# Loading the experts' weights from SyncE's and ScalarE's DMA queues in turn, in place of SyncE's alone

## The chip, the cores and the metric

The kernel runs on one core of one Trainium2 chip. The metric is device time in microseconds (us) of one execution of the whole program. Engines are named as the profile names them: PE is TensorE's matmul (PEld its weight load), DVE is VectorE, ACT is ScalarE, POOL is GpSimd, SP is SyncE. A "q" behind an engine (SPq, ACTq) is the engine's own sequencer, where it waits and where it issues DMAs.

## The reference, cut to what matters

The program computes two transformer blocks on 512 tokens of width 1024. The change touches the first block's feed-forward part, a mixture of 16 experts in which each expert picks its 64 best tokens. All of it is float32.

```python
def expert_choice_ffn(h, w_router, w_gate, w_up, w_down):
    B, N, D = h.shape                               # 1, 512, 1024
    cap = EC_FACTOR * N // N_EXPERTS                # 64 tokens per expert
    aff = jax.nn.softmax((h @ w_router).astype(F32), axis=-1)
    gate, idx = lax.top_k(jnp.swapaxes(aff, 1, 2), cap)
    xg = jax.vmap(lambda hb, ib: hb[ib])(h, idx)
    hid = jax.nn.silu(jnp.einsum('becd,edf->becf', xg, w_gate)) * jnp.einsum('becd,edf->becf', xg, w_up)
    y = jnp.einsum('becf,efd->becd', hid, w_down) * gate[..., None].astype(h.dtype)
    return jax.vmap(lambda yb, ib: jnp.zeros((N, D), yb.dtype).at[ib.reshape(-1)].add(yb.reshape(-1, D)))(y, idx)
```

`w_gate` and `w_up` are 16 x 1024 x 2048 and `w_down` is 16 x 2048 x 1024, so the three hold 384 pieces of one megabyte (MiB).

## The kernel before, in words

**Order of the program.** First come the first block's mixers, the output projection with the router (matmuls `wo`, whose weights are split by ACT at L1812 into `wh` and by DVE at L1813 into `wl`), and the choice of tokens. Then come the experts (function `experts`), and then the second block. A scheduler puts the instructions of each engine into one fixed order, and each engine works through its own list strictly in that order: while an instruction waits for a semaphore, nothing behind it on that engine starts, and that holds for the issue of a DMA too.

**The experts** are taken two at a time, in eight pairs. The text counts the one-megabyte loads from 0 to 383. Pair p (0 to 7) uses loads 48p to 48p+47: 16 of `w_gate`, then 16 of `w_up`, then 16 of `w_down`, the two experts in turn. For one pair, the steps in order are:

1. gather the pair's tokens with matmuls (tile `g`, L1993), which ACT copies to `xg` (L1997); the first half stands before the gate matmuls, the rest among them;
2. 64 gate matmuls (tile `a`, L2025), then ACT applies Silu from PSUM to `hid` (L2038, four instructions);
3. 64 up matmuls (L2025 again, into the same four PSUM banks, so they wait for the Silu), which DVE multiplies into `hid` (L2040);
4. turn `hid` with transposes (L2046) and do 64 down matmuls (tile `y`, L2060);
5. ACT scales the result (`ysb`, L2069, two instructions), PE spreads it over the tokens (`o`, L2076 and L2077), DVE adds it up in `accT` (L2078). PE then gathers for the next pair.

In PE's list the `o` matmuls of a pair stand ahead of all matmuls of the next pair.

**The loads.** `Stream` gives each load the next buffer of a ring: 2 + 9 + 2 + 6 buffers, and one more from the pool `x2`, 20 in all. So load u needs the buffer that load u-20 had, and waits until PE has used that one up. There is a second condition. The landing of every DMA, of whatever queue, is counted on one of eight semaphores (DMAHW0 to DMAHW7) that the DMAs take in turn, and a DMA is issued only after the one eight places before it has landed. Both waits stand on the engine that issues. Before the change that is SP (L93), which has no other work. The second block's loads (L283) are on SP, and a few small ones (L116, L120, L1799, L2128, L2130) are on ACT's queue.

Of the kernel before, what the change touches and what calls it, by code (L numbers as in the profile page):

```python
# [40 lines left out]
class Ring:  # L41

    def __init__(self, *pools):
        self.order = [p for p in pools for _ in range(p[2])]
        self.i = 0
# [38 lines left out]
class Stream:  # L84

    def __init__(self, nc, ring, srcs):
        self.nc, self.ring, self.srcs, self.q = nc, ring, list(srcs)[::-1], []

    def ahead(self, n):
        for _ in range(n):  # L90
            src, a = self.srcs.pop()
            v = self.ring.next().rearrange("p (a b) -> p a b", a=a)
            self.nc.sync.dma_start(v, src)  # L93
            self.q.append(v)

    def next(self):
# [2068 lines left out]
```

## Time and profile before

| | |
|---|---|
| median of 3 runs | 2568.22 us (2567.2 to 2570.2) |
| the profiled execution's own time | 2567.43 us |
| its span, first to last instruction | 2565.7 us |
| mean granted TensorE clock | 0.987 of full speed |
| busy share of the span | PE 96%, PEld 65%, DVE 41%, ACT 27%, POOL 10% |
| bytes read from HBM | 543.56 MB, 213 GB/s over the span |

A share of busy time is an average over stages with different limits. PE's share is high nearly everywhere, because matmuls overlap in the records; what ends a wait in a stage tells more than the share. The experts take the span from about 570 to 1500 us.

### The profile page before, as it was taken

What the parts mean: (1) busy time and instruction counts of PE and PEld (TensorE: products, weight loads), DVE (VectorE), ACT (ScalarE), POOL (GpSimd) and SP (SyncE); (2) the same over time, 40 slices, a digit from 0 to 9 for tenths busy, and PEclk for the clock granted to TensorE, in tenths of its full rate; (3) what the DMA queues carried; (4) which work ended last, traced back from release to release, by engine and by line L of the source; (5) the groups of instructions that cost most, each with busy time, mean ns of one, the idle gap of its engine ahead of it and who ended that gap; (6) DMA issues with size and microseconds to landing.
All of it is one profiled execution on the core that took longest, in us unless ns stands there. A gap on an engine that the chain in (4) does not pass through costs nothing. (4 is left out here: it accounts for less than half of the span.)

```text
span 2565.7 us, 31621 instructions
## 1 busy us (share of the span) xinstructions
PE 2456.9 (96%) x12919; PEld 1660.6 (65%) x12919; DVE 1044.4 (41%) x1871; ACT 691.0 (27%) x1314; POOL 249.3 (10%) x304
## 2 busy tenths in 40 slices
PE   7988999989999999999999999999999999999999
PEld 5768878863434343433434358778888897788887
DVE  5699348633111101010101056744444556644443
ACT  4422337520001000000000045532222355322221
POOL 1344354200000000000000021000000020000000
PEclk9998999989999999999999999999999999999999
DMA  8441110469999999999999943133222221333220
GB/s 274 149 150 34 48 36 18 141 274 419 420 422 421 421 421 421 421 421 422 421 421 421 421 163 99 64 117 94 88 97 76 64 83 50 115 99 99 91 91 33
DMA packets 165432, 547.75 MB, mean 213 GB/s; under 512 B 19183, under 2 KB 100903, under 8 KB 113959
## 3 DMA queue, kind: packets, MB, share of 16 engines
q1 hardware_dynamic: 159120, 544.39, 54.8%
q10 hardware_dynamic: 6167, 1.33, 0.3%
q8 instruction: 102, 1.67, 0.3%
q14 instruction: 43, 0.35, 0.0%
HBM read 543.56 MB, written 2.13 MB: 213 GB/s over the span
## 5 line engine op out<-in xcount | busy, mean ns | idle before, releaser
L2025 PE MATMUL a<-w,xg 128*64 128x512 f32 x2048 | 498.3, 597 | 0.0
L2025 PEld LDWEIGHTS a<-w,xg 128*64 128x64 f32 x2048 | 179.0, 136 | 293.8 <-issue 282.6
L194 ACT ACTIVATE wh<-w 128x512 fp32r<-128x512 f32 (+3 forms) x304 | 202.6, 678 | 457.5 <-PE gu L201 223.5
L2060 PE MATMUL y<-w,hT 128*64 128x512 f32 x1024 | 266.9, 599 | 12.7 <-DMA w<-in_w_down_dram 9.6
L202 PE MATMUL gu<-hh,wl 128*128 128x512 f32 x704 | 278.0, 395 | 0.0
L201 PE MATMUL gu<-hl,wh 128*128 128x512 f32 x704 | 276.4, 393 | 0.0
L200 PE MATMUL gu<-hh,wh 128*128 128x512 f32 x704 | 274.0, 389 | 0.0
L195 DVE TENSOR_TENSOR wl<-w,wh 128x512 fp32r<-128x512 f32 (+3 forms) x304 | 223.6, 748 | 122.6 <-ACT wh L194 122.4
L2060 PEld LDWEIGHTS y<-w,hT 128*64 128x64 f32 x1024 | 90.5, 136 | 171.3 <-issue 131.0
L2040 DVE TENSOR_TENSOR hid<-a,hid 128x512 f32<-128x512 f32 x32 | 21.8, 690 | 331.4 <-PE a L2025 331.1
L201 PEld LDWEIGHTS gu<-hl,wh 128*128 128x128 f32 x704 | 132.5, 188 | 30.9
L200 PEld LDWEIGHTS gu<-hh,wh 128*128 128x128 f32 x704 | 132.5, 188 | 29.5
L202 PEld LDWEIGHTS gu<-hh,wl 128*128 128x128 f32 x704 | 132.7, 188 | 26.5
L2069 ACT ACTIVATE ysb<-y,wt 128x512 fp32r<-128x512 f32 x16 | 11.0, 688 | 505.9 <-PE y L2060 505.1
L200 PE MATMUL dn<-hid,wh 128*128 128x512 f32 x352 | 139.4, 401 | 0.0
L202 PE MATMUL dn<-hid,wl 128*128 128x512 f32 x352 | 137.7, 395 | 0.0
L201 PE MATMUL dn<-hid,wh 128*128 128x512 f32 x352 | 137.1, 394 | 0.0
L732 DVE TENSOR_TENSOR accT<-dn,accT 128x512 f32<-128x512 f32 x96 | 66.1, 690 | 125.8 <-PE dn L202 125.8
L241 POOL MEMSET gg<- 128x256 f32 x1 | 0.3, 312 | 929.0 <-PE y L2060 929.0
L1997 ACT ACTIVATE xg<-g,mT,sc 128x128 f32<-128x128 f32 x64 | 25.9, 454 | 208.2 <-PE g L1993 208.2
L2011 DVE COPY wt<-wt 64x1 f32<-64x1 f32 x16 | 2.5, 156 | 191.8 <-PE wt L2008 191.7
L201 PEld LDWEIGHTS dn<-hid,wh 128*128 128x128 f32 x352 | 66.1, 188 | 17.6 <-DVE hid L722 2.3
(694 smaller groups left out, 4057.0 us busy)
## 6 DMA issues: line engine op xcount, KB each, us to landing
w<-in_w_gate_dram SPq DMA_DIRECT2D x150, 1024.0 KB, 19.8
w<-in_w_up_dram SPq DMA_DIRECT2D x150, 1024.0 KB, 19.8
w<-in_w_down_dram SPq DMA_DIRECT2D x150, 1024.0 KB, 19.8
w<-in_w_mod_dram SPq DMA_DIRECT2D x24, 1024.0 KB, 8.9
w<-in_w_in_dram SPq DMA_DIRECT2D x16, 1024.0 KB, 5.3
w<-in_w_out_dram SPq DMA_DIRECT2D x8, 1024.0 KB, 5.0
wo<-in_w_out_dram SPq DMA_DIRECT2D x4, 1024.0 KB, 9.9
w<-in_w_in_dram SPq DMA_DIRECT2D x4, 576.0 KB, 3.8
```

Source lines behind the costliest of these rows:

```text
L194: nc.scalar.activation(hv, src, AF.Copy)
L195: (eng or nc.vector).tensor_tensor(lv, src, hv.bitcast(F32), op=OP.subtract)
L200: nc.tensor.matmul(out, a[0], b[0], start=start, stop=False)
L201: nc.tensor.matmul(out, a[0], b[1], start=False, stop=False)
L202: nc.tensor.matmul(out, a[1], b[0], start=False, stop=stop)
L732: nc.vector.tensor_tensor(xT[:, d], z, xT[:, d], op=OP.add)
L1997: nc.scalar.activation(xg[:, dd, :], g[:, d, :], AF.Identity, scale=k.sc2[:, dd:dd + 1], bias=k.mT[:, 0, 24 + dd:25 + dd])
L2011: nc.vector.tensor_copy(wt[64 * i:64 * i + 64], tp[64 * i:64 * i + 64, 0, i:i + 1])
L2025: nc.tensor.matmul(acc[f][64 * i:64 * i + 64, :], xg[:, kk, 64 * i:64 * i + 64], us[i][:, 0, f * 512:f * 512 + 512], start=kk == 0, stop=k ...
L2040: nc.vector.tensor_tensor(h, a, h, op=OP.mult)
L2060: nc.tensor.matmul(y[dh][64 * i:64 * i + 64, :], hT[g][:, j, 64 * i:64 * i + 64], us[i][:, r, dh * 512:dh * 512 + 512], start=g + j == 0, ...
L2069: nc.scalar.activation(yh, y[i], AF.Copy, scale=wt)
```

## The change

`Stream.ahead` now issues even loads from SP and odd loads from ACT. Sources, buffers, sizes and the order of the ring stay as they are.

```diff
 class Stream:
 
     def __init__(self, nc, ring, srcs):
-        self.nc, self.ring, self.srcs, self.q = nc, ring, list(srcs)[::-1], []
+        self.nc, self.ring, self.srcs, self.q, self.n = nc, ring, list(srcs)[::-1], [], 0
 
     def ahead(self, n):
         for _ in range(n):
             src, a = self.srcs.pop()
             v = self.ring.next().rearrange("p (a b) -> p a b", a=a)
-            self.nc.sync.dma_start(v, src)
+            (self.nc.sync, self.nc.scalar)[self.n % 2].dma_start(v, src)
+            self.n += 1
             self.q.append(v)
```

The change puts 192 DMA issues into ACT's list, among the work that it had. Lines behind 93 stand one higher in the changed kernel (L1812 is L1813 there). Three places show what that does to the lists.

SP in the middle of the experts, before: five loads in a row and the semaphores that each waits for. `PE` is the buffer, `DMAHW` the landing eight DMAs back.

```order
L93 DMA w<-in_w_gate_dram 128x2048 [waits DMAHW4_49,PE_49]
L93 DMA w<-in_w_gate_dram 128x2048 [waits DMAHW5_49,PE_49]
L93 DMA w<-in_w_gate_dram 128x2048 [waits DMAHW6_49,PE_49]
L93 DMA w<-in_w_gate_dram 128x2048 [waits DMAHW7_49,PE_49]
L93 DMA w<-in_w_gate_dram 128x2048 [waits DMAHW0_49,PE_49]
```

SP at a like place in the changed kernel:

```order
L93 DMA w<-in_w_gate_dram 128x2048 [waits DMAHW4_49,PE_49]
L93 DMA w<-in_w_gate_dram 128x2048 [waits DMAHW6_49,PE_49]
L93 DMA w<-in_w_gate_dram 128x2048 [waits DMAHW0_49,PE_49]
L93 DMA w<-in_w_gate_dram 128x2048 [waits DMAHW2_49,PE_49]
L93 DMA w<-in_w_gate_dram 128x2048 [waits DMAHW4_49,PE_49]
```

SP keeps the even loads and the even semaphores; the odd ones (DMAHW1, 3, 5 and 7) went with the odd loads to ACT, where each still waits for the landing of the load eight before it.

ACT from the Silu of one pair to that of the next, before (`xg`, `oht` and `hid` of pairs 2 and 3):

```order
L2038 ACTIVATE hid<-a 128x16x32 x4
L2069 ACTIVATE ysb<-y,wt 128x512 x2
L1997 ACTIVATE xg<-g,mT,sc_4944 128x128 x8
L2005 ACTIVATE oht<-tp 128x512
L2038 ACTIVATE hid<-a 128x16x32 x4
```

ACT over the same stretch of a pair in the changed kernel:

```order
L2039 ACTIVATE hid<-a 128x16x32 x4
L93 DMA w<-in_w_down_dram 128x2048 x7
L93 DMA w<-in_w_gate_dram 128x2048 x8
L93 DMA w<-in_w_up_dram 128x2048
L2070 ACTIVATE ysb<-y,wt 128x512 x2
L93 DMA w<-in_w_up_dram 128x2048
L1998 ACTIVATE xg<-g,mT,sc_4944 128x128 x4
L93 DMA w<-in_w_up_dram 128x2048 x2
L1998 ACTIVATE xg<-g,mT,sc_4944 128x128 x2
L93 DMA w<-in_w_up_dram 128x2048 x2
L1998 ACTIVATE xg<-g,mT,sc_4944 128x128 x2
L2006 ACTIVATE oht<-tp 128x512
```

Between the Silu and `ysb` of pair p there are now 16 issues, of the odd loads 48p+35 to 48p+65 (the last is the first odd one of the next pair's `w_up`). In the last pair there are only six, all of `w_down`.

ACT ahead of the split of the output projection's weights, before (`posi` and `rows` are small constants, `wr` the router's weights):

```order
L116 DMA rows_6280<-in_g_out_pool_dram 4x128 [waits DMAHW3_49]
L116 DMA rows_6280<-in_b_spatial_dram 8x128 [waits DMAHW4_49]
L120 DMA posi<-in_positions_dram 4x128 [waits DMAHW5_49]
L1799 DMA wr<-in_w_router_dram 128x8x16 [waits DMAHW7_49,DVE_49,PE_49]
L1812 ACTIVATE wh<-wo 128x512 x4
```

ACT at that place in the changed kernel:

```order
L117 DMA rows_6280<-in_b_spatial_dram 8x128 [waits DMAHW5_49]
L121 DMA posi<-in_positions_dram 4x128 [waits DMAHW6_49]
L1800 DMA wr<-in_w_router_dram 128x8x16 [waits DMAHW7_49,DVE_49,PE_49]
L93 DMA w<-in_w_gate_dram 128x2048 [waits DMAHW1_49]
L93 DMA w<-in_w_gate_dram 128x2048 [waits DMAHW3_49]
L93 DMA w<-in_w_gate_dram 128x2048 [waits DMAHW5_49]
L93 DMA w<-in_w_gate_dram 128x2048 [waits DMAHW7_49]
L1813 ACTIVATE wh<-wo 128x512 x4
```

Loads 3, 5, 7 and 9 now stand between the router's load and the four `wh`, and load 9 waits on DMAHW7, which is the landing of `wr`, the DMA eight places before it. In DVE's list the step that uses `wr` (L1803) now stands ahead of the four `wl` of L1813; before, it stood behind them.

## Rows read from the trace of the kernel before

**Rows 1.** The page, 40 equal slices of the span: DMA busy tenths and rate.

```profile
DMA  8441110469999999999999943133222221333220
GB/s 274 149 150 34 48 36 18 141 274 419 420 422 421 421 421 421 421 421 422 421 421 421 421 163 99 64 117 94 88 97 76 64 83 50 115 99 99 91 91 33
```

**Rows 2.** Stretches: PE, PEld, DVE, ACT, POOL busy, clock, DMA share, GB/s.

```profile
550.00:560.00 10.00, 6.72 (x45) 6.06 (x44) 4.68 (x23) 4.95 (x5) 1.12 (x2) 0.82 1.02 427
560.00:565.00 5.00, 4.02 (x18) 3.93 (x18) 5.00 (x23) 0.00 (x0) 3.52 (x5) 0.50 0.11 46
565.00:570.00 5.00, 3.93 (x18) 3.87 (x19) 1.31 (x4) 0.00 (x0) 0.00 (x0) 0.50 0.54 179
...
580.00:590.00 10.00, 10.00 (x60) 5.06 (x59) 0.00 (x0) 0.81 (x2) 0.00 (x0) 1.00 1.01 428
...
1000.00:1100.00 100.00, 96.24 (x410) 40.62 (x407) 12.10 (x19) 7.27 (x15) 0.00 (x0) 1.00 1.01 421
```

**Rows 3.** SP's waits, 600 to 1490 us: total, times, longest.

```profile
SPq L93 <- DMA w<-in_w_up_dram: 238.9, 112, 3.6
...
SPq L93 <- PE a L2025: 28.1, 34, 3.7
```

**Rows 4.** The page's DMA issues: KB each, median us from issue to landing.

```profile
w<-in_w_down_dram SPq DMA_DIRECT2D x150, 1024.0 KB, 19.8
...
w<-in_w_in_dram SPq DMA_DIRECT2D x16, 1024.0 KB, 5.3
```

**Rows 5.** Timeline of SP, around PE's first gate matmul, and at the last loads.

```profile
566.23 0.33 SPq L93 DMA_DIRECT2D w<-in_w_up_dram  x1
...
575.84 0.81 SPq L93 DMA_DIRECT2D w<-in_w_up_dram  x2
...
1441.76 27.64 SPq L93 DMA_DIRECT2D w<-in_w_down_dram  x12
```

**Rows 6.** Timeline of PE: first gate matmuls of pairs 0 and 7.

```profile
572.16 2.37 PE L2025 MATMUL a<-w,xg 128*64 128x512 f32 x10
...
1384.08 2.37 PE L2025 MATMUL a<-w,xg 128*64 128x512 f32 x10
```

**Rows 7.** Timeline of ACT: Silu and `ysb` of pair 0, then pairs 6 and 7.

```profile
604.72 0.60 ACT L2038 ACTIVATE hid<-a 128x512 f32<-128x512 f32 x1 [11.85 <-PE a L2025]
...
665.47 1.50 ACT L2069 ACTIVATE ysb<-y,wt 128x512 fp32r<-128x512 f32 x2 [57.58 <-PE y L2060]
...
1372.53 1.50 ACT L2069 ACTIVATE ysb<-y,wt 128x512 fp32r<-128x512 f32 x2 [73.17 <-PE y L2060]
...
1417.89 1.57 ACT L2038 ACTIVATE hid<-a 128x512 f32<-128x512 f32 x3 [14.41 <-PE a L2025]
...
1491.77 1.50 ACT L2069 ACTIVATE ysb<-y,wt 128x512 fp32r<-128x512 f32 x2 [71.55 <-PE y L2060]
```

**Rows 8.** Timeline of ACT at the router's load and the first `wh`.

```profile
507.36 0.44 ACTq L1799 DMA_DIRECT2D wr<-in_w_router_dram  x1
507.85 2.20 ACT L1812 ACTIVATE wh<-wo 128x512 fp32r<-128x512 f32 x4 [12.43 <-DMA w<-in_w_gate_dram]
```

**Rows 9.** DMA issues, 505 to 520 us: the router's load.

```profile
wr<-in_w_router_dram ACTq DMA_DIRECT2D x1, 64.0 KB, 8.6
```

**Rows 10.** Timeline of DVE: the step that uses `wr`.

```profile
516.09 0.29 DVE L1803 TENSOR_TENSOR wrs<-wr,sc 128x128 f32<-128x128 f32 x1 [4.41 <-DMA wr<-in_w_router_dram]
```

**Rows 11.** Stretches around the router's load, columns as in rows 2.

```profile
505.00:510.00 5.00, 4.67 (x24) 3.59 (x24) 1.91 (x5) 2.15 (x5) 0.88 (x8) 1.00 0.72 260
510.00:515.00 5.00, 3.92 (x22) 3.01 (x20) 1.67 (x3) 3.34 (x7) 0.00 (x0) 1.00 1.02 358
515.00:520.00 5.00, 2.90 (x20) 2.64 (x20) 3.57 (x6) 1.78 (x3) 0.00 (x0) 1.00 0.93 368
```

**Rows 12.** Stretches of 4 us around an idle PE, columns as in rows 2.

```profile
139.00:143.00 4.00, 0.42 (x3) 0.13 (x2) 3.97 (x4) 0.63 (x1) 0.10 (x1) 1.00 0.00 0
143.00:147.00 4.00, 4.00 (x13) 3.21 (x14) 3.94 (x3) 0.59 (x1) 0.00 (x0) 0.57 0.02 4
```

## The prediction

> **What bounds the kernel now.** The slices come first [rows 1]: for fourteen of them, the experts' stage, the DMA engines are full and move 419 to 422 GB/s, and a stretch of 100 us shows the same 421 [rows 2]. PE is busy 96% of that stretch too, so busy shares do not decide. SP's waits do [rows 3]. The row shown is one of three alike, one for each weight matrix (234 to 239 us in 112 to 115 waits each, so 2.1 us a wait): SP waits for the landing of the load eight places back. For a buffer that PE still uses it waits little (28 us in the largest row). So the transfers pace the stage. Twelve issues at its end take 27.64 us; the last lasts 0.33, so eleven steps take 27.31, 2.483 us a load [rows 5]. With eight under way that is 19.9 us from issue to landing, and the row says 19.8 [rows 4].
>
> A pair of experts is 48 loads, 119.2 us. What does PE need for a pair when no weight is late? From `ysb` of pair 6 (1372.53) to the first gate matmul of pair 7 (1384.08) it is 11.55 us [rows 6, 7]. From there to the Silu (1417.89) it is 33.8. From Silu to `ysb` I take pair 0, which still had full buffers: 604.72 to 665.47, 60.75 us. (Pair 7 took 73.9 there, waiting for weights.) The sum is 106.1 us, so PE has 13.1 us a pair to spare.
>
> When does the stream start? The first 20 loads fill the buffers early, and the DMA engines are nearly idle from 560 to 570 (shares 0.11 and 0.54) [rows 2]. Load 19 goes at 566.23, load 20 only at 575.84, when PE has used the first buffers: 3.7 us after its first gate matmul at 572.16 [rows 5, 6]. So the stage ends a fixed 364 loads after PE begins, and whatever moves PE's first gate matmul moves the end one for one. The last load is issued at 1469.07 (1441.76 + 27.31) and lands 19.8 us later, at 1488.9; PE's last `ysb` follows at 1491.77 [rows 7].
>
> **The change, part by part.**
>
> SP loses 192 issues of 0.33 us. Each was covered by the 2.1 us wait beside it, so this is worth nothing. If the wait were gone, SP alone could issue a load every 0.4 us or so [rows 5].
>
> The number of loads under way stays eight, since the eight semaphores are shared; four are now on either queue. The bytes per load stay. The trace has no stretch with two queues of large loads, so the rate is an unknown. The DMA share is 1.01 to 1.02 in full stretches, which leaves no gap for a second queue to fill; the fastest rows are 427 and 428 GB/s against 421 [rows 2]. The other bound is a loss of the same size. One per cent is 9.1 us, because load 20 to the last landing takes 913 us (575.84 to 1488.9). I take 421, no change, to which most rows are nearest; plus and minus 1.7%, 15.5 us, go into the range.
>
> In front of the experts, ACT's four `wh` started at 507.85, 0.05 us after the router's load was out (507.36 + 0.44) [rows 8]. Now loads 3, 5, 7 and 9 stand between, and load 9 waits for the landing of `wr`. That took 8.6 us [rows 9], which is 516.0, and DVE's use of it at 516.09 says the same [rows 10]. With the issue, ACT's `wh` start at about 516.4, 8.5 us late, and behind them stand the rest of the split weights and PE's `wo` matmuls. Part of this stall was there before: from 505 to 520 PE was busy 11.5 of 15 us, idle 3.5 [rows 11], while DVE stood at the same landing for 4.4 us [rows 10]. So PE loses about 8.5 in place of some 2.5 (what of the 3.5 fell at that landing), **+6 us**. The bounds are nothing, if other matmuls fill the gap, and 8.5, if none of the old stall is shared. What is late next is the choice of tokens and PE's first gate matmul, and with it the whole stream: the last landing moves to 1494.9.
>
> In each pair, ACT must issue 16 odd loads between the Silu and `ysb`. The last, 48p+65, is issued only after load 48p+57 has landed. Behind it on ACT stands `ysb`; behind `ysb` wait PE's `o` matmuls and all of the next pair. PE, however, ends the pair with load 48p+47. Before, it did so within 3 us of the landing (1488.9 and 1491.77), so now it must wait until ten more have landed. In pairs 0 to 6 this costs nothing by itself. PE has 13.1 us to spare, and the loads go on: at `ysb` the ten loads 48p+58 to 48p+67 have buffers, 24.8 us of transfers. PE frees the next two buffers 11.55 + 3.7 = 15.2 us later, and a lone 1 MB load takes 5.3 us, 2.8 more than its 2.48 of transfer [rows 4]: 18.0 us, so 6.8 us are left before the engines run dry.
>
> It costs at the end. `ysb` of pair 6 needs load 345, which lands 38 loads before the last: 1494.9 - 94.4 = 1400.5. From there PE has a pair of its own speed to do, 106.1 us: the last `ysb` is at 1506.6 in place of 1491.77. That is 14.8 us, the 6 from the front among them, so **+8.8 us** here. In the last pair only six issues stand ahead of `ysb`, and the last of their loads is down well before PE gets there.
>
> PE's stall before each `ysb`, about 13 us, has a second price. After PE did 0.42 us of work in 4 us, the granted clock was 0.57 in the next 4 us of full work, that is about 3.4 us at 1.2 GHz in place of 2.4 [rows 12]; 560 to 570 was 10 us at 0.50, with pauses [rows 2]. At half speed 3.4 us cost 1.7 and 10 us cost 5. I take **+3 us**, between the two. Only the last stall moves the end; in the others it comes out of the 6.8 us (3.8 are left).
>
> The second block's loads now stand behind small constants on SP. They can go out when SP's last weight load is issued, some 12 us of last-pair work before PE needs them: nothing. Without that cover it would be a landing of 5.3 us.
>
> The sum, on the profiled execution's own 2567.4 us (its span of 2565.7 and 1.7 around it): 6 + 8.8 + 3 = 17.8, so 2585.2. The median of the runs is 0.8 higher, so I say 2586.
>
> **The rivals.**
>
> *The engines run dry at each pair's end.* Same stall, but the 3.8 us do not suffice, because the clock stays low for longer or the two queues end unevenly. Each pair from 0 to 6 then adds what is missing; 3 us in each is 21 us, and the time is 2607. For it speaks how little is left; against it that this is a margin and not a deficit in every row I have.
>
> *The rate rises a little.* At 428, the best row, the stream is 15.5 us shorter and the time 2570: no change. What speaks for it is that this rate occurs, against it that it occurs only for 10 us and that the engines are full already.
>
> *Faster.* The same mechanism at a higher rate: two queues keep each engine fed so that it goes beyond any row here. It decides from 2.5% on (23 us, 432 GB/s); at 3% the time is 2559. The shares of 1.01 speak against it, and nothing in the trace for it. The Trainium skill's page "DMA: Bandwidth & Descriptors", section "Issuing engines are not separate DMA queues", has a rule against it: DMAs of all issuing engines run on the same 16 DMA engines and interleave, and a second issuer saves only issue time. By that rule the gain in rate is nothing and the sum stays 2586; the full shares in the rows agree. The same page's section "Where 436 GB/s comes from" puts the ceiling at 435 GB/s; an estimate from it is 3.3% above 421, 30 us, so 2556 at the best.
>
> **How the numbers follow.** A difference of over 0.2%, 5 us, is about what this measurement can tell from none. My forecast has a chance of 0.64 (from 2576, with nothing lost in front and a short spell at the low clock, to 2596, with a loss of 1% in the rate), the dry engines 0.15, no change 0.13, faster 0.08. So slower has 0.79. The range of 2567 to 2607 leaves out the faster case, a part of the no-change case and the worse half of the dry one.
>
> **What would show it.** In the changed profile, the first gate matmul should start at about 578 and the four `wh` at 516. The waits should name a long wait of PE's `o` matmuls (or of DVE's `yl`) for ACT's `ysb`, and ACT's own wait there should be for a weight load, not for PE. The step between first gate matmuls should stay at 119 us in the middle pairs, with 421 GB/s; the last landing should lie some 12 to 15 us before the last `ysb`, not 3. Wrong would be a rate off 421 by over 1%, gaps in the DMA row at the pairs' ends, or a `wr` that lands much later behind two busy queues.

## The result, and the profile after

The changed kernel takes 2589.84 us (median of 4 runs, 2586.93 to 2591.52), against 2567.71 for the kernel before (2565.48 to 2570.2): a ratio of 1.0087, 95% interval 1.0074 to 1.0099, so 22 us slower. Its profiled execution took 2588.92 us with a span of 2587.2, 21.5 more than before.

The page after, 40 slices, answers to [rows 1]:

```profile
DMA  8441110559999999999999942132222221333220
GB/s 274 148 146 37 45 36 17 199 211 376 421 421 422 420 422 421 421 421 421 421 422 421 420 159 82 64 114 87 95 98 88 65 82 50 114 98 96 86 96 33
```

The rate in the stage is what it was; the plateau only begins later. A stretch of 100 us shows the same, columns as in [rows 2], and PE busy less:

```profile
1000.00:1100.00 100.00, 84.22 (x404) 35.02 (x402) 12.94 (x20) 7.37 (x15) 0.00 (x0) 0.91 1.01 421
```

Where PE stands is in the waits, 490 to 585 us and then 600 to 1500 us (total, times, longest):

```profile
PE wo L201 <- ACT wh L1813: 16.2, 1, 16.2
DVE wrs L1804 <- DMA wr<-in_w_router_dram: 15.7, 1, 15.7
...
ACT ysb L2070 <- DMA w<-in_w_gate_dram: 500.7, 7, 73.5
PE o L2077 <- ACT ysb L2070: 97.5, 7, 16.0
```

Both places that the prediction named are there. The front, in ACT's timeline, beside [rows 8], and DVE's step beside [rows 10]:

```profile
502.53 0.42 ACTq L1800 DMA_DIRECT2D wr<-in_w_router_dram  x1
502.99 15.87 ACTq L93 DMA_DIRECT2D w<-in_w_gate_dram  x4
518.90 2.19 ACT L1813 ACTIVATE wh<-wo 128x512 fp32r<-128x512 f32 x4 [28.31 <-DVE wrs L1804]
...
518.60 0.29 DVE L1804 TENSOR_TENSOR wrs<-wr,sc 128x128 f32<-128x128 f32 x1 [15.65 <-DMA wr<-in_w_router_dram]
```

The row of `wh` names DVE's `wrs` as what ended ACT's idle time; `wrs` waited for `wr` too, and an experiment below shows `wh` going ahead of it. Four odd loads stand between `wr` and `wh`, and the fourth goes out only when `wr` has landed, after 16.0 us and not the 8.6 of [rows 9] (the DMA issues of 500 to 520 us):

```profile
wr<-in_w_router_dram ACTq DMA_DIRECT2D x1, 64.0 KB, 16.0
```

The tail, in ACT's and PE's timelines at the end of pair 6 and of pair 7:

```profile
1406.53 0.34 ACTq L93 DMA_DIRECT2D w<-in_w_up_dram  x1
1406.99 1.27 ACT L2070 ACTIVATE ysb<-y,wt 128x512 fp32r<-128x512 f32 x2 [72.45 <-DMA w<-in_w_gate_dram]
1511.80 1.50 ACT L2070 ACTIVATE ysb<-y,wt 128x512 fp32r<-128x512 f32 x2 [57.52 <-PE y L2061]
...
1384.51 8.32 PE L2061 MATMUL y<-w,hT 128*64 128x512 f32 x38
1407.73 1.22 PE L2077 MATMUL o<-oht,ysb 128*128 128x512 f32 x2 [14.90 <-ACT ysb L2070]
```

PE ends pair 6 at 1392.83 and stands 14.9 us: load 353 goes out at 1406.53, when load 345 has landed, and only then ACT computes `ysb`.

To say where the 21.5 us lie I cut each profiled execution at three instants: the last `ch` matmul, the last PE work ahead of the place where the two orders part; the first gate matmul; the last `ysb`. These are PE's rows, of after, then of before:

```profile
489.31 0.60 PE L1712 MATMUL ch<-c,qd 128*128 128x128 f32 x4
583.81 6.66 PE L2026 MATMUL a<-w,xg 128*64 128x512 f32 x30
```

```profile
494.13 0.60 PE L1711 MATMUL ch<-c,qd 128*128 128x128 f32 x4
```

The fourth of the four matmuls starts at 489.63 and 494.46. Up to there nothing was changed, but in this execution that part was 4.8 us shorter. From there to the first gate matmul it is 94.2 us against 77.7 (the **front**, +16.5); from there to the last `ysb` 928.0 against 919.6 (the **stage**, +8.4); behind it 1075.4 against 1073.9 (+1.5). The sum, -4.8 + 16.5 + 8.4 + 1.5, is 21.6. In the eleven further profiles the last `ch` lies between 488.4 and 496.1 and the part behind the last `ysb` takes 1071.8 to 1077.6, so spans of single executions differ by some us for no reason of this study's. Front and stage repeat far better, and the experiments are read by them.

### The profile page after: what moved, and what is told of

The parts are those of the page before. It is cut to its first block, busy times and chain, and to the rows that moved or that the text cites. A ratio compares the mean times of both kernels' runs of the same rounds, so it can differ in the third digit from the quotient of the medians.

```text
span 2587.2 us, 31613 instructions
## 1 busy us (share of the span) xinstructions
PE 2382.1 (92%) x12919; PEld 1615.9 (62%) x12919; DVE 1045.8 (40%) x1871; ACT 691.0 (27%) x1314; POOL 249.7 (10%) x304
## 4 chain that ended last, share of the span: by engine, by line
PE 69%; DMA 18%; DVE 8%; ACT 2%; issue 1%; POOL 1%; ACTq 0%; POOLq 0%; SPq 0%; DVEq 0%
PE a L2026 13%; DMA w<-in_w_gate_dram 10%; PE gu L203 6%; PE gu L202 6%; PE gu L201 6%; DMA w<-in_w_down_dram 6%; PE dn L201 3%; PE dn L202 3%; PE dn L203 3%; PE g L1994 3%; PE y L2061 2%; PE ATz L1628 2%; PE wo L201 1%; PE wo L202 1%; PE wo L203 1%; DMA w<-in_w_mod_dram 1%
## 5 line engine op out<-in xcount | busy, mean ns | idle before, releaser
L2026 PE MATMUL a<-w,xg 128*64 128x512 f32 x2048 | 453.5, 594 | 0.0
L2026 PEld LDWEIGHTS a<-w,xg 128*64 128x64 f32 x2048 | 146.3, 137 | 281.7 <-issue 276.5
L2061 PE MATMUL y<-w,hT 128*64 128x512 f32 x1024 | 225.0, 594 | 2.8 <-DVE hT L2049 2.8
L2061 PEld LDWEIGHTS y<-w,hT 128*64 128x64 f32 x1024 | 71.4, 137 | 139.8 <-issue 132.9
L2077 PE MATMUL o<-oht,ysb 128*128 128x512 f32 x64 | 38.4, 625 | 103.6 <-ACT ysb L2070 97.5
L2077 PEld LDWEIGHTS o<-oht,ysb 128*128 128x128 f32 x64 | 15.4, 255 | 131.9 <-ACT ysb L2070 103.8
L2071 DVE SCALAR_TENSOR_TENSOR yl<-y,wt,ysb 128x512 fp32r<-128x512 f32 x16 | 11.5, 747 | 184.3 <-ACT ysb L2070 184.3
## 6 DMA issues: line engine op xcount, KB each, us to landing
w<-in_w_gate_dram ACTq DMA_DIRECT2D x64, 1024.0 KB, 19.8
w<-in_w_down_dram ACTq DMA_DIRECT2D x64, 1024.0 KB, 17.4
```

Of the source, the lines that this page charges most:

```text
L2026: nc.tensor.matmul(acc[f][64 * i:64 * i + 64, :], xg[:, kk, 64 * i:64 * i + 64], us[i][:, 0, f * 512:f * 512 + 512], start=kk == 0, stop=k ...
L2061: nc.tensor.matmul(y[dh][64 * i:64 * i + 64, :], hT[g][:, j, 64 * i:64 * i + 64], us[i][:, r, dh * 512:dh * 512 + 512], start=g + j == 0, ...
L2077: nc.tensor.matmul(o, ysb[:, d * P:d * P + P], oht, start=True, stop=False)
```

## The experiments

All change which queue a load takes in `ahead`, where `self.n` is the load's number, or where `wr` is loaded. Medians stand against the kernel before on the same chip (2568.75, 2567.34 and 2566.88 us in the three sets, single runs from 2560 to 2577).

**Each half undone, and both.** Loads 0 to 19 from SP:

```
-            (self.nc.sync, self.nc.scalar)[self.n % 2].dma_start(v, src)
+            (self.nc.sync, self.nc.scalar)[self.n % 2 if self.n >= 20 else 0].dma_start(v, src)
```

> The changed kernel, but loads 0 to 19 (those that fill the buffers in front of the experts) all go out from SP; from load 20 on every second one goes out from ACT as in the change. Theory A (ACT stands in order, in two places): in front ACT's four `wh` start about 0.1 us after `wr` is issued, as before, and the wait of PE's `wo` matmuls for them is gone; the stalls ahead of `ysb` stay. So what is left is the part inside the stage, first gate matmul to last `ysb` 928 us as in the changed kernel (919.6 before): 2577 us, between 2572 and 2580. Rival B (the second queue itself makes every load slower, or the pairs carry the whole loss): no gain, 2588 to 2590. Rival C (the front carries it all, the stage nothing): 2568.

Measured: 2576.67 us, ratio 1.0036 (1.0022 to 1.0050). Front 77.7, stage 929.2; `wr` lands in 8.5 us.

The last pair's loads from SP, `self.n % 2 if self.n < 336 else 0`:

> The changed kernel, but loads 336 to 383 (the last pair's) all go out from SP; the front and pairs 0 to 5 are as changed. Theory A: the `ysb` of pair 6 no longer waits for a landing, PE reaches the last pair in time to follow the transfers again, first gate matmul to last `ysb` falls from 928 to about 920 us, the last landing lies about 3 us before the last `ysb`: 2581 us. The stalls of pairs 0 to 5 stay in the trace, 9 to 15 us each, and cost nothing. Rival B (every pair's stall costs a little, or the rate): 48 loads of 384 are undone, an eighth of 8.4 us at most, 2588 to 2589.

Measured: 2580.71 us, 1.0052 (1.0036 to 1.0069). Front 94.0, stage 919.4. ACT's `ysb` of pairs 5, 6 and 7 in its timeline:

```profile
1291.79 1.26 ACT L2070 ACTIVATE ysb<-y,wt 128x512 fp32r<-128x512 f32 x2 [70.99 <-DMA w<-in_w_gate_dram]
1397.58 1.52 ACT L2070 ACTIVATE ysb<-y,wt 128x512 fp32r<-128x512 f32 x2 [57.53 <-PE y L2061]
1508.46 1.50 ACT L2070 ACTIVATE ysb<-y,wt 128x512 fp32r<-128x512 f32 x2 [64.30 <-PE y L2061]
```

The `ysb` of pair 5 still waits for a weight, that of pair 6 for PE, and the whole 8.4 us are back. The six stalls that remain cost nothing, as the prediction had it.

Both, `self.n % 2 if 20 <= self.n < 336 else 0`:

> Both at once: loads 0 to 19 and 336 to 383 from SP, the 316 between them alternate. Theory A: as before, 2568 us (2565 to 2571), though two queues carry 82 per cent of the loads and PE still stalls 9 to 15 us ahead of six `ysb`; the DMA row stays at 419 to 422 GB/s. Rival B (the second queue or the low clock after each stall costs something in every pair): six sevenths of 8.4 us or more remain, 2575 or above. Rival D (two queues move more than one when nothing stands in the way): below 2565.

Measured: 2568.36 us, 1.0009 (0.9996 to 1.0022), no change. Front 77.6, stage 920.0. A stretch of it, two queues at work and PE stalling:

```profile
1100.00:1200.00 100.00, 83.19 (x402) 34.39 (x400) 13.75 (x21) 4.97 (x11) 0.00 (x0) 0.91 1.01 421
```

So the loss is made in the front and at the last pair's start, and neither the second queue nor the low clock behind each stall costs anything in between. By the medians the front costs 13.2 us (2589.84 less 2576.67) or 12.4 (2580.71 less 2568.36), by the traces 16.4. With runs that spread like this I can't say where 3 to 4 us go; the traces agree among themselves: the three with the whole front show 94.0 to 94.2, those without it 77.6 to 78.0 (79.4 in one).

**Half of the tail.** Loads 352 to 383 from SP, `self.n % 2 if self.n < 352 else 0`:

> The changed kernel, but loads 352 to 383 go out from SP. The last load that ACT issues ahead of the `ysb` of pair 6 is then 351, not 353, so its wait ends with the landing of load 343, two loads or 5.0 us earlier. Theory A: first gate matmul to last `ysb` 923 us (928 in the changed kernel), the wait of PE's `o` matmuls for that `ysb` 5 us shorter than for those before it; 2585 us. Rival F (a threshold: the tail is lost or it is not): 928 and 2590, or 920 and 2581.

Measured: 2588.39 us, 1.0077 (1.0064 to 1.0091); stage 923.8, 4.2 less than the changed kernel. The stage says that the price grows with the number of landings ACT stands for: this one step in between costs half, and rival F's threshold is out. The median fell by 1.5 only, within the spread, and decides nothing.

**Which wait is it in front?** `wr` early, in a tile of its own, all odd loads from ACT:

```
-        nc.scalar.dma_start(wr[:, :, 0:16], I['w_router'][0].rearrange("(k p) e -> p k e", p=P))
...
+        k.wr = pk.tile([P, 8, 32], F32, name="wr")
+        nc.sync.dma_start(k.wr[:, :, 0:16], I['w_router'][0].rearrange("(k p) e -> p k e", p=P))
```

> The changed kernel, but the router's weights `wr` lie in a tile of their own that is loaded at the program's start, so nothing waits for that landing. Loads 3, 5, 7 and 9 still stand ahead of three of the four `wh` on ACT. Theory A (any landing eight places back costs as much): load 9 now waits for load 1, which lands with eight loads under way; the three `wh` are held to about 518 as before and PE's first gate matmul is no earlier than 580; 2588 us. Rival G (it is the small rows of `wr` behind two queues that land late): ACT goes on within 4 us, the first gate matmul is at 570 to 574, and 2577 us is left, as with loads 0 to 19 from SP.

Measured: 2574.22 us, 1.0022 (1.0009 to 1.0034). Front 77.0, stage 928.3. Rival G holds: ACT's timeline shows four loads out in 1.91 us.

```profile
505.31 1.91 ACTq L93 DMA_DIRECT2D w<-in_w_gate_dram  x4
507.26 1.68 ACT L1812 ACTIVATE wh<-wo 128x512 fp32r<-128x512 f32 x3 [1.33 <-issue]
```

My reason for A was wrong too: with `wr` gone, the DMA eight places ahead of load 9 is the small `posi`, not load 1. The run therefore took away both ACT's long stand and the late `wr`. The next kernel parts them: load 9 alone from SP, `self.n % 2 if self.n != 9 else 0`.

> The changed kernel, but load 9 alone, the one that waits on ACT for the landing of `wr`, goes out from SP. ACT is then free for its four `wh`; loads 2 to 8 still go out within some 5 us beside `wr`, and `wr` still lands late. Theory A, as the prediction told it (ACT's stand behind load 9 is the price in front): the four `wh` start at most 4 us after `wr` is issued, from the last `ch` matmul to the first gate matmul it is about 78 us as before (94 in the changed kernel), and the time is 2577 us. Rival G (the late `wr` is the price): DVE stands for `wr` some 15 us by itself, `wl` stands behind that on DVE, PE's `wo` matmuls wait for `wl` in place of `wh`; from `ch` to the gate matmul still 91 us or more, and the time is 2587 to 2590.

Measured: 2589.25 us, 1.0094 (1.0079 to 1.0108). Front 90.7, stage 928.2. `wr` lands in 13.7 us. The timelines of ACT, DVE and PE:

```profile
504.83 0.42 ACTq L1800 DMA_DIRECT2D wr<-in_w_router_dram  x1
505.29 1.88 ACTq L93 DMA_DIRECT2D w<-in_w_gate_dram  x3
507.21 2.19 ACT L1813 ACTIVATE wh<-wo 128x512 fp32r<-128x512 f32 x4 [14.33 <-issue]
...
518.60 0.29 DVE L1804 TENSOR_TENSOR wrs<-wr,sc 128x128 f32<-128x128 f32 x1 [13.60 <-DMA wr<-in_w_router_dram]
518.81 2.49 DVE L1814 TENSOR_TENSOR wl<-wo,wh 128x512 fp32r<-128x512 f32 x4
...
507.90 0.50 PE L201 MATMUL wo<-mix,wh 128*128 128x512 f32 x1 [2.23 <-ACT wh L1813]
...
519.54 0.80 PE L203 MATMUL wo<-mix,wl 128*128 128x512 f32 x1 [10.93 <-DVE wl L1814]
```

ACT is free and has its four `wh` out by 509.4, yet PE stands all the same, for DVE's `wl`, which is behind `wrs` on DVE. So the price in front is the late landing of `wr` with DVE's new order behind it, and not ACT's stand. That stand adds little: the front is 3.5 us shorter here (94.2 less 90.7), but `wr` also landed 2.3 us sooner, so about 1.2 are left for it. The medians, 0.6 us apart, can't tell such amounts.

That `wr` is late because of the loads beside it is what its durations suggest. In the changed kernel and here seven loads (2 to 8) go out within some 2 us of `wr`; before and with loads 0 to 19 from SP (8.6 and 8.5 us) only loads 2 and 3 do, and load 4 follows 6.6 us after `wr`. Seven loads of 2.483 us are 17.4 us, against 16.0 and 13.7. The changed kernel has an eighth, load 10, which SP sends 4.9 us after `wr`; here SP stands at load 9 and sends load 10 only behind the landing. SP's timelines, of the changed kernel and of this one:

```profile
502.57 5.23 SPq L93 DMA_DIRECT2D w<-in_w_gate_dram  x5
...
504.87 14.46 SPq L93 DMA_DIRECT2D w<-in_w_gate_dram  x6
```

One load more is 2.483 us and the two landings differ by 2.3. This is an estimate, since no run varied the number by itself.

**The same two queues without ACT.** GpSimd's queue, which has no work in the stage, `(self.nc.sync, self.nc.gpsimd)[self.n % 2 if self.n >= 20 else 0]`:

> The changed kernel with GpSimd's queue in ACT's place: loads 0 to 19 from SP, from load 20 on every second one from POOL, which has no work of its own in the experts' stage. Its loads take turns on eight semaphores of their own, so up to sixteen can be under way in place of eight. Theory A (what costs is that the issues stand ahead of ACT's compute): no stall ahead of `ysb`, first gate matmul to last `ysb` as before, 919 to 921 us, 2568 us. Rival B (a second queue costs by itself): 2577 or above, as with loads 0 to 19 alone undone. Rival D (more under way, or two queues, raise the rate): above 425 GB/s in the middle slices and below 2562.

Measured: 2573.49 us, 1.0022 (1.0011 to 1.0032). Front 77.8, stage 927.8: no wait for `ysb`, as theory A has it, and still 8.2 us lost. Nearly all of them are lost in the last pair, in DVE's and PE's timelines:

```profile
1491.98 0.23 DVE L164 TENSOR_TENSOR cv<-cv 128x64 f32<-128x64 f32 x1 [20.45 <-DMA cv<-in_g_k_head_dram]
...
1493.12 0.68 DVE L2049 COPY hT<-tp 128x512 f32<-128x512 f32 x1
...
1493.86 8.58 PE L2061 MATMUL y<-w,hT 128*64 128x512 f32 x32 [8.44 <-DVE hT L2049]
```

With half the loads off SP, the second block's constants stand elsewhere in the order: DVE takes one (`cv`) ahead of the last `hT`, while its rows come late. SP's issues of these constants are 5 us apart there, two landings each. The changed kernel has that order too:

```profile
1501.57 0.22 DVE L164 TENSOR_TENSOR cv<-cv 128x64 f32<-128x64 f32 x1 [9.77 <-DMA cv<-in_g_k_head_dram]
...
1503.61 0.69 DVE L2049 COPY hT<-tp 128x512 f32<-128x512 f32 x1
...
1498.60 13.96 PE L2061 MATMUL y<-w,hT 128*64 128x512 f32 x64
```

Its last `hT` is done at 1504.3, and PE comes to need it after half of its 64 matmuls, at 1505.6, so there it cost nothing, by 1.3 us. The prediction left DVE's order out of its sum. With loads 336 to 383 from SP, the last `hT` is ahead of `cv` again:

> As the kernel with GpSimd's queue, but loads 336 to 383 go out from SP; from GpSimd only every second one of loads 20 to 335. In the run with GpSimd's queue throughout, no `ysb` waited for a landing, yet 8 us came back in the last pair: DVE stood there 20.5 us for a constant of the second block (`cv`, its `g_k_head` rows), and behind it in DVE's order stood the last `hT`, for which PE waited 8.4 us. In this kernel DVE has that constant behind the last `hT` again. Theory A: 919 to 921 us from the first gate matmul to the last `ysb`, 2565 to 2569 us. Rival B (sixteen loads under way, or GpSimd's queue, cost by themselves): 2573 as there.

Measured: 2565.67 us, 0.9996 (0.9984 to 1.0007), no change; front 79.4, stage 919.6. So a second queue is free where nothing has to stand behind its waits.

**Fewer loads on ACT.** Only odd `w_down` loads, `self.n % 2 if self.n % 48 >= 32 else 0`:

> Only every second load of `w_down` goes out from ACT (loads 33, 35, ... 47 of each pair, 64 of 384); all else from SP, so the front is untouched. On ACT these eight stand behind the Silu of their own pair and ahead of its `ysb`; the last needs the landing of load 39, long before PE ends the pair with load 47. Theory A (what counts is whether the landing that ACT stands for comes after PE's own last weight): no wait of PE for `ysb`, steps of 119 us, 2568 us (2565 to 2571). Rival B (the price goes with the number of loads that ACT issues): a third of the changed kernel's 8.4 us in the stage, 2571 to 2572. Rival E (the loads behind the Silu go out late and the DMA engines have gaps): middle slices under 419 GB/s and 2575 or more.

Measured: 2574.22 us, 1.0028 (1.0016 to 1.0040); front 78.0, stage 923.0. Theory A missed: no `ysb` holds PE, but the rate dips, in four stretches of 20 us (two shown):

```profile
720.00:740.00 20.00, 19.56 (x84) 7.20 (x80) 2.07 (x4) 0.00 (x0) 0.00 (x0) 1.00 1.00 409
...
1420.00:1440.00 20.00, 20.00 (x87) 7.81 (x84) 0.00 (x0) 2.17 (x4) 0.00 (x0) 1.00 0.96 390
```

This is rival E, at less than its price: now the loads stand behind ACT's compute, and go out late. Without them in the last pair, `self.n % 48 >= 32 and self.n < 336`:

> The kernel with every second `w_down` load on ACT, but none in the last pair (56 loads from ACT). There the stage was 923.0 us, 3.4 over before, and the transfers had four dips: 409, 405, 412 and 390 GB/s in stretches of 20 us, which is 0.6 + 0.8 + 0.4 + 1.5 = 3.3 us, the largest in the last pair, where ACT sends load 369 only after the Silu. If the dips are the price, the one in the last pair goes: the stage is 921 to 922 us and the time about 2570. If something else in the last pair was the price: 919.6 and 2567.

Measured: 2568.77 us, 1.0006 (0.9994 to 1.0018); stage 920.1. Three dips are still there (406, 410 and 402 GB/s), and 2.9 of the 3.4 us are gone: what was lost in the last pair counted nearly alone. So the dips in earlier pairs are not priced as I had added them up; this is inconclusive between my two cases, and nearer to the second.

**A faster version.** The kernel before with `wr` early, all loads from SP:

> The kernel before, with `wr` loaded at the program's start into a tile of its own and all weights from SP. With the changed kernel the early `wr` gave 77.0 us from the last `ch` matmul to the first gate matmul against 77.7 before, so the old wait for `wr` is worth 0.7 us: 2567 us, no change that can be measured. If the 3.5 us that PE stood idle at that place all come back: 2564.

Measured: 2559.72 us, 0.9973 (0.9963 to 0.9983): 0.27% faster than the kernel before. Front 74.2 in place of 77.7, and PE has no idle time around the router's load (it was 3.5 us in [rows 11]):

```profile
505.00:510.00 5.00, 5.00 (x26) 4.02 (x25) 1.94 (x6) 2.00 (x4) 1.43 (x8) 1.00 0.64 217
510.00:515.00 5.00, 5.00 (x27) 4.09 (x27) 3.94 (x7) 3.72 (x8) 0.00 (x0) 1.00 0.92 387
515.00:520.00 5.00, 5.00 (x34) 4.48 (x33) 3.49 (x7) 2.65 (x5) 0.00 (x0) 1.00 0.97 362
```

The first case, 0.7 us, is missed: it took the old wait for `wr` from a kernel that has two queues in front and loses time there in other places too (77.0 against 74.2 here). The trace shows the 3.5 us of the second case; the rest of the 7.2 between the medians I could not place.

## Why the prediction was right, and where it was not

*The bound* was right. The transfers pace the stage at 421 GB/s whatever sends them, and taking issues off SP gave nothing; the seven steps between first gate matmuls take 119.4 us in the mean (583.81 to 1419.27). The Trainium skill's page "DMA: Bandwidth & Descriptors", section "Issuing engines are not separate DMA queues", says that a second issuer saves only issue time; the two kernels with no change, at 421 GB/s on two queues, agree. The rivals that needed another rate, or engines that run dry at the pairs' ends, are both out: all middle slices show 420 to 422.

*The front, +6*, named the right landing and mis-sized the term: it was 16.5. The step that failed is "load 9 waits for the landing of `wr`. That took 8.6 us": beside two queues it took 16.0, 7.4 more. The prediction named this as a thing that would make it wrong, but kept it out of the sum. The next step failed with it, "PE loses about 8.5 in place of some 2.5". PE stood 16.2 us where it had been idle 3.5, so it lost 12.7 and not 6. PE's rows of before, around its old stand:

```profile
508.53 0.51 PE L200 MATMUL wo<-mix,wh 128*128 128x512 f32 x1 [0.33 <-ACT wh L1812]
...
517.10 0.50 PE L200 MATMUL wo<-mix,wh 128*128 128x512 f32 x1 [3.18 <-DVE accT L1866]
```

Of the 12.7, 7.4 are the later landing and some 5.3 the order: before, PE had its first matmuls with `wh` and `wl` to do ahead of that wait, and now ACT's `wh` and DVE's `wl` both stand behind it. With load 9 on SP only DVE's do, and PE still stood 13.2 us (2.23 and 10.93), with `wr` 2.3 us earlier. The lists ahead of the prediction show DVE's new order, but its sum followed ACT only. No run has the late landing with DVE's old order, so the 7.4 and the 5.3 remain an estimate.

The rest of the front's 16.5 us is the clock, for which the prediction had no term there. These are stretches of after (columns as in [rows 2]) and PE's rows for the choice of tokens (`affr`) and the first gather (`g`), then a stretch and the same rows of before:

```profile
519.60:524.40 4.80, 4.80 (x13) 3.83 (x14) 3.21 (x5) 3.46 (x7) 0.00 (x0) 0.50 1.02 423
562.00:572.00 10.00, 6.50 (x30) 5.46 (x29) 5.65 (x28) 4.95 (x5) 2.17 (x4) 0.50 0.51 175
568.10 1.94 PE L1914 MATMUL affr<-c,aff 128*128 128x128 f32 x8 [1.11 <-DVE aff L1890]
577.83 6.05 PE L1994 MATMUL g<-oh,xn 128*128 128x128 f32 x32 [1.07 <-DVE oh L1986]
...
556.00:560.00 4.00, 1.83 (x13) 1.37 (x11) 1.89 (x9) 2.17 (x3) 0.10 (x1) 0.93 1.01 422
558.11 1.06 PE L1913 MATMUL affr<-c,aff 128*128 128x128 f32 x8 [1.34 <-DVE aff L1889]
566.96 5.28 PE L1993 MATMUL g<-oh,xn 128*128 128x128 f32 x32 [1.07 <-DVE oh L1985]
```

The clock fell while PE stood (0.52 from 507 to 519 us). Behind the stand PE worked 4.8 us at half the clock, 1.2 GHz, which costs 2.4 (an estimate). `affr` ran at 1.2 GHz too and took 0.9 more than before, where the stretch around it has 0.93. From the first `g` to the first gate matmul it is 5.98 us in place of 5.20; the clock is 0.50 there from 572 to 582 us, and before it was 1.00 from 570 on, so I count these 0.8 to it as well. 12.7 + 2.4 + 0.9 + 0.8 is 16.8, near the 16.5. Why the clock stays low for longer ahead of the experts is not shown; the kernel with `wr` early and two queues has the slow `affr` too (1.94 us), the one with `wr` early and SP alone has not (1.06).

*The tail, +8.8*, was right in place and near in size: 8.4 in the trace with the clock's part in it, all of it back when the last pair's loads leave ACT. The predicted `ysb` of pair 6, 1400.5, moved by the 5.7 us that the first gate matmul came later than forecast (583.81 in place of 578.2), is 1406.2; it came at 1406.99. The last pair was faster than forecast: from its first gate matmul (1419.27) to its `ysb` it took 92.5 us, where the prediction has 33.8 + 60.75 = 94.6, and the 33.8 is from a pair that the loads paced.

*The clock, +3*, stood in the wrong place. Around the last stall (stretches, columns as in [rows 2]):

```profile
1394.00:1412.00 18.00, 3.86 (x8) 2.19 (x8) 3.34 (x5) 1.27 (x2) 0.00 (x0) 0.53 1.01 422
1412.00:1420.00 8.00, 7.57 (x45) 5.18 (x46) 3.90 (x6) 1.43 (x4) 0.00 (x0) 1.00 1.01 420
```

The granted clock is 0.53, near 1.2 GHz, in the stretch in which PE mostly stands, and 1.00, 2.4 GHz, in the next, in which it works again. From `ysb` to the gate matmul it took 12.28 us in place of 11.55, 0.7 and not 3. In front the clock took some 4 (2.4 + 0.9 + 0.8), for which the prediction had nothing.

*The sum* came out near, 2586 against 2589.8, in part by luck, because misses met: in the profiled execution +10.5 in front, -3.4 for tail and clock there together (8.4 in place of 8.8 + 3), -4.8 in the untouched early part and +1.5 at the end.

## What to carry to other kernels

An issue on an engine that computes puts that issue's waits, for a buffer and for an older landing, ahead of all later work of the engine; count which landing the next activation comes to stand for, and compare it with the last one that the work needs by itself. When the transfers are the bound, such stalls are free until the last one, so look at the end and the start of the stream. A small load that compute waits for should go out before the queue fills, and moving loads between queues can also change a scheduler's order on engines that the diff never names.

## What the runs showed of the hardware that was not expected

A load of 64 KB landed in 8.5 us with two 1 MB loads sent right behind it, in 13.7 us with seven, and in 16.0 with seven and an eighth 4.9 us later. GpSimd's DMAs are counted on eight semaphores of their own (111 to 118 in that kernel's trace; those of SP and ACT are 100 and 102 to 108), so with its queue up to sixteen loads can be under way. A load then took 34.5 us from issue to landing in place of 19.8, at the same 421 GB/s; at 2.483 us a load that is some fourteen under way in place of eight. These are that kernel's DMA issues, beside [rows 4]:

```profile
w<-in_w_down_dram POOLq DMA_DIRECT2D x64, 1024.0 KB, 34.5
```
